# Four edits to a two-layer decoder trunk: where the index queries are split, what S3 is summed from, how fast weight sums are issued, where residual rows are scaled

## The chip, the cores and the metric

The kernel runs on one core of a Trainium2 chip. The metric is the device time of one execution, in microseconds (us). Five engines with an instruction queue each matter here: TensorE (PE in the profile; PEld are its weight loads), VectorE (DVE), ScalarE (ACT), GpSimd (POOL) and SyncE (SP). Each engine works through its own queue in order; an instruction whose semaphore has not come blocks everything queued behind it on that engine. Transfers are issued by SP (queue q1 in the profile) and by POOL (queue q0) and are carried out by the same 16 DMA engines.

## The reference

Two layers (DEPTH = 2) over 512 positions of width 2048, all in float32:

```python
h = jnp.einsum('bsd,dn->bsn', x, w_in)              # one projection, its columns split in groups
q_idx = rope(iq.reshape(b, s, 16, 64), pos)         # indexer: 16 query heads, one key head
k_idx = rope(ik.reshape(b, s, 1, 64), pos)[:, :, 0, :]
rel   = relu(einsum('bqhi,bki->bqhk', q_idx, k_idx) * 64 ** -0.5)
score = einsum('bqhk,bqh->bqk', rel, w_idx)         # the 128 best keys of a query are attended to
y = concatenate([y_fox * silu(fg), y_dsa * silu(dg), y_mem * silu(mg)])
x = layer_norm(ALPHA * x + y @ w_out, ln_gain, ln_bias)
```

y_fox is causal attention with a forget bias (6 heads), y_dsa attention over the chosen keys (6 heads), y_mem attention into 256 memory tokens (4 heads). Value, gate and some query columns (5120 of them) and the output projection are by far the largest products.

## The kernel before

Every float32 product is made of three TensorE matmuls: both operands are split into a high and a low part (`split`, L216: ACT copies the high part, `whi`; DVE subtracts to get the low part, `wlo`), and high*high, low*high and high*low are accumulated (`product`, L221, L225 to L227). The weights come in chunks of 128 x 2048 floats, 1 MB each, through six half-chunk buffers `raw`; each half chunk is split once, three halves ahead of its use, into four buffers.

The order of a layer is written out: `mv` and `mk` (memory values and keys), `small` (index key, index weights, forget logits), eight `iq` chunks (two index heads each), 70 `vs` chunks (values), 16 chunks of heads, 28 `out` chunks. An `iq` chunk has 48 matmuls of 384 columns, a `vs` chunk 24 of 512.

The values are a seven-product scheme on 2 x 2 blocks (`PRODUCTS`): P1 = A11 B11, P7 = S3 T3, Q6 = S2 T2, and so on. The left sums S3 = A11 - A21, S2, S1, S4 are made on the core from x (`val_operands`, `val_sum` L848, `val_hi` L853, `val_lo` L859). The right sums T1 to T4 are sums of weight blocks; T3 and part of T1 are made in DRAM by transfers that POOL issues (`weight_sums`: a first copy, L425, then an accumulating transfer, L405, 1 MB each) and loaded later as `raw<-sum`. T2 and T4 are grown in the raw buffers of T3, the first by an accumulating transfer of POOL (`grow_w`, L284), the second by DVE (`make_w`, L294). Ten chunks per column pair come first (P1 P1 P7 P7 P2 Q6 Q6 P2 Q4 Q4, five pairs), then four per pair (Q5 Q5 Q3 Q3).

All other work is in generators that `begin` starts and `tick` advances: once in the middle and once at the end of a chunk, except that those started with `whole=True` skip the middle of `vs` and `out` chunks. So a generator that yields 1 runs at every tick, one that yields 2 at every second one. `paced` decides how many ticks lie between two weight sums, by stage. Outside the value stage each weight sum is preceded by `pool_waits`: DVE writes a mark and POOL reads it, so that POOL can't run ahead. Inside the value stage there is no mark.

After an `iq` chunk, `index_rope` turns the rows (ACT moves four quarters, L588; DVE multiplies, L589 and L590; POOL subtracts, L591), then ACT copies the high part of each of the two heads (L1296) and DVE subtracts (L1297). `index_scores` does one head per tick, from two ticks later: six matmuls (`ix`), three `rel` on ACT (L685), three `acc` on DVE (L691).

Between the layers `next_x` normalises z, transposes it for the next layer (`xf`, `xh`, `xl`; L1034 on DVE and POOL in turns) and stores rows of the residual x1; `residual_rows` in the value stage of the second layer loads rows of x1, multiplies by gain, adds bias (L1052, L1053) and stores them again.

Of the kernel before, what the change touches and what calls it, by code (L numbers as in the profile page):

```python
# [14 lines left out]
ALU = mybir.AluOpType  # L15
# [162 lines left out]
def kernel(  # L178
# [171 lines left out]
    def split_x(k):  # L350
        hi, lo = slot("xh", F32R), slot("xl", F32R)
        split(x_raw.pop(k), hi, lo)
        xT[k] = (hi, lo)

# [73 lines left out]
    def paced(gen, steps=2):  # L428

        n = 0  # L430
        for _ in gen:
            n += 1
            while now[1] == "kv":
                yield 1
            yield {"heads": 1, "out": 3, "index": 1}.get(now[1], steps)
# [10 lines left out]
    def all_sums():  # L446


        for l in range(DEPTH):
            yield from paced(value_sums(l), 1)  # L450
# [218 lines left out]

    def index_scores(l):  # L670
# [189 lines left out]

    def val_operands():
# [3 lines left out]
        for i in range(4):  # L865
            val_sum("S3", i, ((a11, 0, add), (a21, 0, sub), (a11, 1, add), (a21, 1, sub)))
            yield 1
            val_hi("S3", i)
            yield 1
            val_lo("S3", i)  # L870
# [143 lines left out]
    def next_x():  # L1014
# [9 lines left out]
        for k in range(KT):  # L1024
# [10 lines left out]
            xT[k] = (hi, lo)  # L1035
            if k % 2:
                for st in (o - 1, o) if 0 < c < 3 else ():
                    store(st, c - 1)
                if k == 13:
                    load_row(0, 2, nc.sync)  # L1040
                yield 1
        for c in (2, 3):
            for st in range(4):
                if (st, c) == (1, 2):
                    load_row(0, 3, nc.sync)
                scale_row(z[st, c], c)
                store(st, c)
                yield 1
            del rows["g", c], rows["b", c]

    def scale_row(t, c):
        nc.vector.tensor_tensor(t, t, rows["g", c], op=ALU.mult)  # L1052
        nc.vector.tensor_tensor(t, t, rows["b", c], op=ALU.add)  # L1053

    def residual_rows(l):

        tiles = [(st, c) for c in range(2) for st in range(4)]
        t = {}
        for n in range(len(tiles) + 1):
            if n:  # L1060
                st, c = tiles[n - 1]
                d = t.pop(n - 1)
                scale_row(d, c)
# [81 lines left out]
    for i, (kind, l, j, col, _) in enumerate(chunks):  # L1145
# [143 lines left out]
        elif kind == "iq":  # L1289
            t = index_rope(ps, P, P, nc.gpsimd)  # L1290

            for e in range(2):
                s = slot("iqs", F32R)
                r, o = (slice(0, 64), slice(64, 128)) if e == 0 else (slice(64, 128), slice(0, 64))
                c = slice(P, SEQ)
                nc.scalar.activation(s[r, c], t[r, c], AF.Copy)  # L1296
                nc.vector.tensor_tensor(s[o, c], t[r, c], s.bitcast(F32)[r, c], op=ALU.subtract)  # L1297
                idx["q", 2 * j + e] = s
            if j == 0:
                begin(index_scores(l), 2, last=True, whole=True)  # L1300
            if j == 2:
                begin(val_operands(), 2, last=True)
# [149 lines left out]
```

## Time and profile before

| what | us |
|---|---|
| median of 3 runs (lowest to highest) | 1953.41 (1953.16 to 1954.32) |
| profiled execution, its time | 1953.65 |
| its span, first to last instruction | 1951.8 |
| PE busy | 1905.0 (98%) |
| DVE busy | 1475.0 (76%) |
| ACT busy | 1015.8 (52%) |
| POOL busy | 367.4 (19%) |
| all transfers | 499.35 MB |

A busy PE is not PE at full speed: matmuls overlap, and the granted clock (PEclk, 1.00 is full speed) can be lower. The share of the DMA engines is the time that packets took over the time of 16 engines, so it can be a little over 1.

In the span, layer 0 has its `iq` chunks from about 60 to 145 us and its values from there to about 545; layer 1 has them from about 1040 to 1125 and to about 1505.

### The profile page before, as it was taken

How to read it: one execution, taken by the hardware profiler on the slowest of the kernel's cores; microseconds unless marked ns; L12 is line 12 of the kernel's file. 1: busy time of each engine (PE TensorE's matmuls, PEld its weight loads, DVE VectorE, ACT ScalarE, POOL GpSimd, SP SyncE). 2: the span in 40 equal slices, each digit the busy share in tenths (PEclk: the TensorE clock that was granted, in tenths of full speed). 3: DMA queues.
4: the chain of work that ended last, by engine and by line, in shares of the span. 5: the costliest groups of instructions: out<-in, count | busy, mean ns of one | idle time of the engine just before them, and what ended most of it. 6: DMA issues, size and time to landing. Idle time of an engine off the chain costs nothing.

```text
span 1951.8 us, 26382 instructions
## 1 busy us (share of the span) xinstructions
PE 1905.0 (98%) x9250; PEld 1616.7 (83%) x9250; DVE 1475.0 (76%) x2422; ACT 1015.8 (52%) x1598; POOL 367.4 (19%) x618
## 2 busy tenths in 40 slices
PE   9998899999999999999999989999999999999997
PEld 8996678888888888888899968888888888888886
DVE  5788477777955676789787887898877466767888
ACT  5665244445455554555474664444554565455453
POOL 0223111111122122110042221111212220112101
PEclk9999899999999999999999989999999999999999
DMA  9899886688987789798888997877999886889965
GB/s 342 285 282 237 271 253 181 181 225 265 342 275 223 233 249 278 227 335 270 299 251 283 283 220 222 252 238 210 230 278 340 265 241 201 263 252 252 348 199 152
DMA packets 168115, 499.35 MB, mean 256 GB/s; under 512 B 16865, under 2 KB 61921, under 8 KB 159085
## 3 DMA queue, kind: packets, MB, share of 16 engines
q1 hardware_dynamic: 131724, 294.19, 44.4%
q0 software_dynamic: 36256, 203.47, 40.8%
q8 instruction: 73, 1.20, 0.2%
q14 instruction: 62, 0.50, 0.1%
HBM read 451.43 MB, written 174.09 MB: 320 GB/s over the span
## 4 chain that ended last, share of the span: by engine, by line
PE 81%; DVE 10%; ACT 3%; DMA 3%; issue 2%; POOL 1%; SPq 0%; DVEq 0%; ACTq 0%; POOLq 0%
PE v L226 12%; PE v L227 12%; PE v L225 12%; PE c L227 8%; PE c L225 7%; PE c L226 7%; PE z L226 4%; PE z L227 4%; PE z L225 4%; DVE wlo L219 3%; DMA raw<-in_wall_dram 2%; DVE acc L691 1%; DMA raw<-sum 1%; ACT whi L218 1%; DVE vx L848 1%
## 5 line engine op out<-in xcount | busy, mean ns | idle before, releaser
L219 DVE TENSOR_TENSOR wlo<-raw,whi 128x1024 fp32r<-128x1024 f32 (+1 forms) x521 | 636.0, 1225 | 272.8 <-ACT whi L218 270.7
L218 ACT ACTIVATE whi<-raw 128x1024 fp32r<-128x1024 f32 (+1 forms) x521 | 548.0, 1054 | 438.8 <-PE v L227 247.3
L225 PE MATMUL c<-xh,whi 128*128 128x512 f32 (+1 forms) x800 | 301.4, 377 | 0.6 <-ACT rel L685 0.6
L227 PE MATMUL c<-xh,wlo 128*128 128x512 f32 (+1 forms) x800 | 298.4, 373 | 0.0
L226 PE MATMUL c<-xl,whi 128*128 128x512 f32 (+1 forms) x800 | 297.8, 372 | 0.0
L226 PE MATMUL v<-wlo,vxh 128*128 128x512 f32 x640 | 249.4, 390 | 2.3 <-DVE wlo L219 2.3
L225 PE MATMUL v<-whi,vxh 128*128 128x512 f32 x640 | 249.7, 390 | 1.2 <-ACT whi L218 1.2
L227 PE MATMUL v<-whi,vxl 128*128 128x512 f32 x640 | 249.1, 389 | 0.0
L226 PE MATMUL v<-wlo,xh 128*128 128x512 f32 x480 | 192.7, 401 | 11.8 <-DVE wlo L219 7.6
L225 PE MATMUL v<-whi,xh 128*128 128x512 f32 x480 | 191.3, 399 | 9.9 <-ACT whi L218 9.9
L227 PE MATMUL v<-whi,xl 128*128 128x512 f32 x480 | 191.3, 399 | 0.0
L226 PE MATMUL z<-wlo,yh 128*128 128x512 f32 (+1 forms) x434 | 168.1, 387 | 2.5 <-DVE wlo L219 2.5
L225 PE MATMUL z<-whi,yh 128*128 128x512 f32 (+1 forms) x434 | 168.4, 388 | 0.0
L227 PEld LDWEIGHTS c<-xh,wlo 128*128 128x128 f32 x800 | 150.1, 188 | 21.9
L225 PEld LDWEIGHTS c<-xh,whi 128*128 128x128 f32 x800 | 150.3, 188 | 21.5 <-ACT rel L685 1.2
L227 PE MATMUL z<-whi,yl 128*128 128x512 f32 (+1 forms) x434 | 167.8, 387 | 0.0
L226 PEld LDWEIGHTS c<-xl,whi 128*128 128x128 f32 x800 | 150.4, 188 | 20.6
L396 POOL TENSOR_TENSOR seen<-mark,mhalf 128x1 f32<-128x1 f32 x107 | 28.0, 261 | 700.2 <-DVE mark L395 689.5
L226 PEld LDWEIGHTS v<-wlo,vxh 128*128 128x128 f32 x640 | 120.1, 188 | 27.9 <-DVE wlo L219 3.2
L225 PEld LDWEIGHTS v<-whi,vxh 128*128 128x128 f32 x640 | 120.1, 188 | 27.2 <-ACT whi L218 2.3
L227 PEld LDWEIGHTS v<-whi,vxl 128*128 128x128 f32 x640 | 120.1, 188 | 25.0
L226 PEld LDWEIGHTS v<-wlo,xh 128*128 128x128 f32 x480 | 92.8, 193 | 33.7 <-DVE wlo L219 14.4
(226 smaller groups left out, 3207.6 us busy)
## 6 DMA issues: line engine op xcount, KB each, us to landing
raw<-in_wall_dram SPq DMA_DIRECT2D x322, 512.0 KB, 7.4
sum<-in_wall_dram POOLq DMA_DIRECT2D x60, 1024.0 KB, 11.6
raw<-sum SPq DMA_DIRECT2D x120, 512.0 KB, 6.4
v<-vraw POOLq DMA_DIRECT2D x120, 256.0 KB, 6.3
raw<-in_wall_dram POOLq DMA_DIRECT2D x48, 512.0 KB, 8.0
vraw<-v SPq DMA_DIRECT2D x80, 256.0 KB, 6.6
other<-in_wall_dram SPq DMA_DIRECT2D x48, 256.0 KB, 9.1
x<-z POOLq DMA_DIRECT2D x24, 256.0 KB, 5.6
```

The source lines that it names most:

```text
L218: nc.scalar.activation(hi, src, AF.Copy)
L219: nc.vector.tensor_tensor(lo, src, hi.bitcast(F32), op=ALU.subtract)
L225: nc.tensor.matmul(ps, ah, bh, start=start, stop=False, skip_group_check=more)
L226: nc.tensor.matmul(ps, ah, bl, start=False, stop=False, skip_group_check=more)
L227: nc.tensor.matmul(ps, al, bh, start=False, stop=stop, skip_group_check=more)
L396: nc.gpsimd.tensor_tensor(seen, mark, mhalf, op=ALU.mult)
L691: nc.vector.scalar_tensor_tensor(a, rel, wq, a, op0=ALU.mult, op1=ALU.add)
L848: nc.vector.tensor_tensor(d, acc, x, op=op)
```

## The change

- `index_parts` is new: the ACT copies and DVE subtractions of the two index heads leave the end of the `iq` chunk and come as a generator with a wait of 1, at the tick in the middle of the next chunk.
- `first_sum` is new: S3 is one subtraction per 256 columns from the unsplit x (`xraw` in layer 0, `xf` in layer 1), issued where x is split. Before, it was summed from the split parts in `val_operands`, three operations per 256 columns. Its high and low parts come from `first_operands`, started after the first `iq` chunk; `val_operands` (S2 first) starts after the last `iq` chunk, not the third.
- Weight sums for the values: one per two ticks instead of one per tick, in the index and in the value stage. The pace in the heads and out stages stays.
- `next_x` stores all 16 tiles of x1 unscaled, the last four over two ticks; `residual_rows` scales all 16 and not 8, and starts at the first pair's second Q6 chunk and not the second pair's, ten chunks earlier.

```diff
@@ -349,8 +349,10 @@
 
     def split_x(k):
         hi, lo = slot("xh", F32R), slot("xl", F32R)
-        split(x_raw.pop(k), hi, lo)
+        x = x_raw.pop(k)
+        split(x, hi, lo)
         xT[k] = (hi, lo)
+        first_sum(k, x)
 
     load_w(0, 4)
     load_w(1, 2)
@@ -432,7 +434,7 @@
             n += 1
             while now[1] == "kv":
                 yield 1
-            yield {"heads": 1, "out": 3, "index": 1}.get(now[1], steps)
+            yield {"heads": 1, "out": 3, "index": 2}.get(now[1], steps)
 
     def value_sums(l):
 
@@ -447,7 +449,7 @@
 
 
         for l in range(DEPTH):
-            yield from paced(value_sums(l), 1)
+            yield from paced(value_sums(l))
             while now != (l, "heads"):
                 yield 1
             yield from paced(weight_sums("out", l, ("T3", "T1", "T2", "T4"), range(2)))
@@ -667,6 +669,17 @@
                                     pattern=[[-1, P]], channel_multiplier=1)
         yield 1
 
+    def index_parts(j, t):
+
+        for e in range(2):
+            s = slot("iqs", F32R)
+            r, o = (slice(0, 64), slice(64, 128)) if e == 0 else (slice(64, 128), slice(0, 64))
+            c = slice(P, SEQ)
+            nc.scalar.activation(s[r, c], t[r, c], AF.Copy)
+            nc.vector.tensor_tensor(s[o, c], t[r, c], s.bitcast(F32)[r, c], op=ALU.subtract)
+            idx["q", 2 * j + e] = s
+        yield 1
+
     def index_scores(l):
         acc = [slot("acc", w=w) for w in BANK_W]
         kh2, kl2 = idx["k"]
@@ -858,16 +871,26 @@
         t = vx[name, i] if name == "S3" else vx.pop((name, i))
         nc.vector.tensor_tensor(lo, t, hi.bitcast(F32), op=ALU.subtract)
 
+    def first_sum(k, x):
+
+        i, e = divmod(k, 2)
+        if i < 4:
+            if e == 0:
+                vx["S3", i] = slot("vx")
+            nc.vector.tensor_tensor(vx["S3", i][:, e * 256:(e + 1) * 256], x[:, 0:256], x[:, 256:512],
+                                    op=ALU.subtract)
+
+    def first_operands():
+        for i in range(4):
+            val_hi("S3", i)
+            yield 1
+            val_lo("S3", i)
+            yield 1
+
     def val_operands():
         add, sub = ALU.add, ALU.subtract
         a11, a12, a21, a22 = (0, 0), (0, 1), (1, 0), (1, 1)
 
-        for i in range(4):
-            val_sum("S3", i, ((a11, 0, add), (a21, 0, sub), (a11, 1, add), (a21, 1, sub)))
-            yield 1
-            val_hi("S3", i)
-            yield 1
-            val_lo("S3", i)
         for i in range(4):
             val_sum("S2", i, (("S3", 0, add), (a22, 0, add), (a22, 1, add)), vx.pop(("S3", i)))
             yield 1
@@ -1033,34 +1056,26 @@
             eng = nc.gpsimd if k % 2 else nc.vector
             eng.tensor_tensor(lo, xf, hi.bitcast(F32), op=ALU.subtract)
             xT[k] = (hi, lo)
+            first_sum(k, xf)
             if k % 2:
-                for st in (o - 1, o) if 0 < c < 3 else ():
+                for st in (o - 1, o) if c else ():
                     store(st, c - 1)
-                if k == 13:
-                    load_row(0, 2, nc.sync)
                 yield 1
-        for c in (2, 3):
-            for st in range(4):
-                if (st, c) == (1, 2):
-                    load_row(0, 3, nc.sync)
-                scale_row(z[st, c], c)
-                store(st, c)
+        for st in range(4):
+            store(st, 3)
+            if st % 2:
                 yield 1
-            del rows["g", c], rows["b", c]
-
-    def scale_row(t, c):
-        nc.vector.tensor_tensor(t, t, rows["g", c], op=ALU.mult)
-        nc.vector.tensor_tensor(t, t, rows["b", c], op=ALU.add)
 
     def residual_rows(l):
 
-        tiles = [(st, c) for c in range(2) for st in range(4)]
+        tiles = [(st, c) for c in range(4) for st in range(4)]
         t = {}
         for n in range(len(tiles) + 1):
             if n:
                 st, c = tiles[n - 1]
                 d = t.pop(n - 1)
-                scale_row(d, c)
+                nc.vector.tensor_tensor(d, d, rows["g", c], op=ALU.mult)
+                nc.vector.tensor_tensor(d, d, rows["b", c], op=ALU.add)
                 nc.gpsimd.dma_start(x1_d[st * P:(st + 1) * P, c * 512:(c + 1) * 512], d)
                 if st == 3:
                     del rows["g", c], rows["b", c]
@@ -1289,17 +1304,12 @@
         elif kind == "iq":
             t = index_rope(ps, P, P, nc.gpsimd)
 
-            for e in range(2):
-                s = slot("iqs", F32R)
-                r, o = (slice(0, 64), slice(64, 128)) if e == 0 else (slice(64, 128), slice(0, 64))
-                c = slice(P, SEQ)
-                nc.scalar.activation(s[r, c], t[r, c], AF.Copy)
-                nc.vector.tensor_tensor(s[o, c], t[r, c], s.bitcast(F32)[r, c], op=ALU.subtract)
-                idx["q", 2 * j + e] = s
+            begin(index_parts(j, t), 1)
             if j == 0:
                 begin(index_scores(l), 2, last=True, whole=True)
-            if j == 2:
-                begin(val_operands(), 2, last=True)
+                begin(first_operands(), last=True)
+            if j == 7:
+                begin(val_operands(), 3, last=True)
             if j == 7:
                 index_tabs.clear()
         if kind in ("fk", "dk"):
@@ -1316,7 +1326,7 @@
             now = (l, "values")
         if kind == "vs" and (name, pair, col) == ("Q6", 0, 1):
             begin(top_keys(l), whole=True)
-        if kind == "vs" and (name, pair, col) == ("Q6", 1, 1) and l > 0:
+        if kind == "vs" and (name, pair, col) == ("Q6", 0, 1) and l > 0:
             begin(residual_rows(l), whole=True)
         if kind == "vs" and (name, col) == ("Q3", 1) and pair > 1:
             if pair == 2:
```

With the change, one chunk of the index stage of layer 0 reads so on DVE. In these rows `wlo` is the low part of a weight half chunk, `iqs` an index head's low part, `acc` the scores of 256, 384 and 512 keys, `vx` the sum S3, `vxl` its low part, `rope` the rotation. Before, from the two `iqs` of the fifth `iq` chunk on:

```order
L1297 TENSOR_TENSOR iqs_1400<-rope_1391,iqs_1400 64x384
L1297 TENSOR_TENSOR iqs_1403<-rope_1391,iqs_1403 64x384
L395 COPY mark_1406<-mhalf 128x1
L691 SCALAR_TENSOR_TENSOR acc_1014<-rel_1421,iw_845,acc_1014 128x256
L691 SCALAR_TENSOR_TENSOR acc_1013<-rel_1424,iw_845,acc_1013 128x384
L691 SCALAR_TENSOR_TENSOR acc_1015<-rel_1427,iw_845,acc_1015 128x512
L859 TENSOR_TENSOR vxl_1361<-vx_1297,vxh_1360 128x512
L848 TENSOR_TENSOR vx_1431<-xh_503 128x256
L848 TENSOR_TENSOR vx_1431<-vx_1431,xl_504 128x256 x2
L848 TENSOR_TENSOR vx_1431<-xh_507 128x256
L848 TENSOR_TENSOR vx_1431<-vx_1431,xl_508 128x256 x2
L219 TENSOR_TENSOR wlo_1444<-raw_1307,whi_1443 128x1024
```

And with the change, in the middle of the fourth `iq` chunk, from a weight half chunk on:

```order
L219 TENSOR_TENSOR wlo_1174<-raw_1039,whi_1173 128x1024
L679 TENSOR_TENSOR iqs_1201<-rope_1132,iqs_1201 64x384
L679 TENSOR_TENSOR iqs_1204<-rope_1132,iqs_1204 64x384
L704 SCALAR_TENSOR_TENSOR acc_1013<-rel_1216,iw_857,acc_1013 128x256
L704 SCALAR_TENSOR_TENSOR acc_1012<-rel_1219,iw_857,acc_1012 128x384
L704 SCALAR_TENSOR_TENSOR acc_1014<-rel_1222,iw_857,acc_1014 128x512
L872 TENSOR_TENSOR vxl_1166<-vx_557,vxh_1165 128x512
L219 TENSOR_TENSOR wlo_1227<-raw_1169,whi_1226 128x1024
L591 TENSOR_TENSOR rope_1254<-c_1168,tab_715 128x384
L592 TENSOR_TENSOR rope_1255<-rope_1255,tab_717 128x384
L397 COPY mark_1270<-mhalf 128x1
L704 SCALAR_TENSOR_TENSOR acc_1013<-rel_1284,iw_857,acc_1013 128x256
```

The six `vx` additions are gone from this place, and the two `iqs` stand behind a weight half chunk and no longer right behind the rotation that they read.

The second place is POOL in the value stage of layer 0, at the end of the first column pair. `sum` from `16x16384` is the first copy of a weight sum, `sum` from `128x2048` the accumulating transfer, `v` a store of values. Before:

```order
L425 DMA sum_2127<-in_wall_dram 16x16384
L425 DMA sum_2166<-in_wall_dram 16x16384
L425 DMA sum_2207<-in_wall_dram 16x16384
L956 DMA v_163<-vraw_2201 128x512
L956 DMA v_163<-vraw_2074 128x512
L956 DMA v_163<-vraw_2204 128x512
L956 DMA v_163<-vraw_2076 128x512
L405 DMA sum_2078<-in_wall_dram 128x2048
L956 DMA v_162<-vraw_2248 128x512
L956 DMA v_162<-vraw_2250 128x512
L405 DMA sum_2127<-in_wall_dram 128x2048
L405 DMA sum_2166<-in_wall_dram 128x2048
```

With the change:

```order
L427 DMA sum_2102<-in_wall_dram 16x16384
L979 DMA v_163<-vraw_2137 128x512
L979 DMA v_163<-vraw_2001 128x512
L979 DMA v_163<-vraw_2140 128x512
L979 DMA v_163<-vraw_2003 128x512
L407 DMA sum_1512<-in_wall_dram 128x2048
L979 DMA v_162<-vraw_2182 128x512
L979 DMA v_162<-vraw_2184 128x512
L407 DMA sum_1630<-in_wall_dram 128x2048
L979 DMA v_162<-vraw_1871 128x512
L979 DMA v_162<-vraw_1873 128x512
```

Around the same eight stores there are three sums and not seven, and the runs of sums with nothing between them are gone. All 28 sums of the layer are still issued, the last of them some 40 value chunks into the stage and not some 12.

The third place is DVE between the layers, where `next_x` splits the new x (`xl`). Before:

```order
L1034 TENSOR_TENSOR xl_9313<-xf_9311,xh_9312 128x512
L219 TENSOR_TENSOR wlo_9333<-raw_9268,whi_9332 128x1024
L1034 TENSOR_TENSOR xl_9355<-xf_9353,xh_9354 128x512
L219 TENSOR_TENSOR wlo_9371<-raw_9328,whi_9370 128x1024
L1034 TENSOR_TENSOR xl_9393<-xf_9391,xh_9392 128x512
```

With the change:

```order
L1057 TENSOR_TENSOR xl_9265<-xf_9263,xh_9264 128x512
L880 TENSOR_TENSOR vx_9269<-xf_9263 128x256
L880 TENSOR_TENSOR vx_9269<-xf_9276 128x256
L219 TENSOR_TENSOR wlo_9288<-raw_9220,whi_9287 128x1024
L1057 TENSOR_TENSOR xl_9310<-xf_9308,xh_9309 128x512
L880 TENSOR_TENSOR vx_9314<-xf_9308 128x256
```

Two subtractions of S3 stand now behind every second `xl`, eight per layer.

## The prediction

> **What bounds the kernel now.** I read the table of stages first (busy time of each engine, granted clock, share of the DMA engines, rate), because the page shows PE busy for 98% of the span and the question is where the rest is lost.
>
> ```profile
> core 0: us, PE busy (x) PEld busy (x) DVE busy (x) ACT busy (x) POOL busy (x), PEclk, DMA share, GB/s
> 80.00:145.00 65.00, 65.00 (x377) 63.50 (x376) 54.00 (x113) 42.70 (x80) 20.75 (x32) 1.00 0.94 274
> 145.00:190.00 45.00, 36.92 (x155) 29.21 (x155) 39.38 (x67) 27.91 (x47) 15.83 (x24) 0.92 0.97 234
> 190.00:262.00 72.00, 58.55 (x221) 44.56 (x220) 34.52 (x50) 20.98 (x23) 11.57 (x16) 0.91 0.95 269
> 262.00:400.00 138.00, 138.00 (x611) 114.25 (x610) 112.58 (x162) 63.37 (x68) 19.05 (x30) 1.00 0.70 204
> 1070.00:1152.00 82.00, 73.00 (x371) 65.89 (x371) 67.29 (x128) 51.76 (x97) 21.28 (x35) 0.94 0.93 260
> 1152.00:1232.00 80.00, 80.00 (x356) 66.45 (x355) 64.46 (x92) 40.56 (x49) 14.07 (x21) 1.00 0.81 210
> 1232.00:1330.00 98.00, 98.00 (x434) 81.13 (x433) 85.17 (x125) 44.64 (x48) 20.16 (x32) 1.00 0.83 249
> ```
>
> PE is full in most stages; three lose time, and those are where the change works. Idle plus clock deficit: 145 to 190 us loses 8.1 + 45 x 0.08 = 11.7 us, 1070 to 1152 us loses 9.0 + 82 x 0.06 = 13.9 us. From 190 to 262 us I count matmuls, all of one width there: 611 in 138 us is 0.226 us each, so 221 are 49.9 us of work and 22.1 us are lost. Together 47.7 us, the most that can be won here.
>
> Second, who makes PE wait in the two stretches, 140 to 265 us and 1050 to 1155 us:
>
> ```profile
> PE v L225 <- ACT whi L218: 10.9, 6, 4.3
> PE v L226 <- DVE wlo L219: 7.1, 7, 2.8
> PE v L226 <- DVE mark L395: 2.1, 1, 2.1
> ...
> PE ix L680 <- DVE iqs L1297: 3.9, 3, 1.7
> PE v L226 <- DVE wlo L219: 2.8, 1, 2.8
> ```
>
> So PE waits for split weights: in layer 1 for DVE, in layer 0 also for ACT's half. Third, the chain of waits between 185 and 262 us, with its two longest pieces, says why ACT was late there:
>
> ```profile
> 191.49 19.84 DMA raw<-in_wall_dram
> ...
> 226.94 23.62 DMA raw<-sum
> ```
>
> There the weights themselves arrived late. Two causes, then: DVE before 190 us and in layer 1, transfers from 190 to 262 us.
>
> **The change part by part.** *Index stage, DVE.* The groups of 75 to 165 us (count, busy us, mean ns, idle before them):
>
> ```profile
> L219 DVE TENSOR_TENSOR wlo<-raw,whi 128x1024 fp32r<-128x1024 f32 x16 | 19.5, 1218 | 1.8 <-ACT whi L218 1.8
> L691 DVE SCALAR_TENSOR_TENSOR acc<-rel,iw,acc 128x512 f32<-128x512 f32 x12 | 8.9, 745 | 0.0
> L1297 DVE TENSOR_TENSOR iqs<-rope,iqs 64x384 fp32r<-64x384 f32 x16 | 8.9, 554 | 14.3 <-ACT iqs L1296 14.1
> L1296 ACT ACTIVATE iqs<-rope 64x384 fp32r<-64x384 f32 x16 | 8.4, 524 | 21.8 <-POOL rope L591 21.6
> L848 DVE TENSOR_TENSOR vx<-vx,xl 128x256 f32<-128x256 f32 x18 | 7.7, 425 | 0.6
> L691 DVE SCALAR_TENSOR_TENSOR acc<-rel,iw,acc 128x384 f32<-128x384 f32 x12 | 7.3, 611 | 0.0
> L691 DVE SCALAR_TENSOR_TENSOR acc<-rel,iw,acc 128x256 f32<-128x256 f32 x12 | 5.7, 475 | 0.0
> L589 DVE TENSOR_TENSOR rope<-c,tab 128x384 f32<-128x384 f32 x8 | 4.4, 550 | 0.8 <-ACT rope L588 0.8
> L590 DVE TENSOR_TENSOR rope<-rope,tab 128x384 f32<-128x384 f32 x8 | 4.4, 546 | 0.0
> L848 DVE TENSOR_TENSOR vx<-xh 128x256 f32<-128x256 f32 x8 | 3.3, 418 | 0.0
> L859 DVE TENSOR_TENSOR vxl<-vx,vxh 128x512 fp32r<-128x512 f32 x4 | 2.7, 685 | 0.0
> ```
>
> PE needs 60 matmuls per `iq` chunk (48, and 6 for each of two heads): 60 of 377 in 65 us is 10.3 us. DVE needs two `wlo` (2.44), rotation (1.10), two `iqs` (1.11), two rounds of `acc` (3.66): 8.3 us. From the fourth chunk on, S3 adds six `vx` (2.54) and a `vxl` (0.69), and every chunk adds 14.3 / 8 = 1.8 us of waiting at `iqs`, since DVE stands behind ACT, which stands behind POOL: 13.3 us against 10.3. DVE falls some 3 us behind per chunk until the four buffers of split weights are used up, near 145 us.
>
> The change takes 24 of these `vx` (24 x 0.42 = 10.1 us) out of each layer's index stage and puts the `iqs` pair half a chunk (5 us) later, behind a `wlo`, when POOL's 1 us subtraction is long done. What is left is 8.3 us, 9.0 while `vxl` lasts: below 10.3, so DVE no longer falls behind. S2 (16 additions and four low parts of 0.69, about 9.5 us) now starts only in the second value chunk. DVE there per chunk: 2.44 + 1.83 (last heads) + 1.7 (S2) + 0.69 = 6.6 us, against 24 matmuls and one head, 5.4 + 1.0 = 6.4; it starts with full buffers, so nothing is lost. The first operands of Q6 are ready about one chunk (5.4 us) before use; if that cover were gone, each of Q6's four half chunks could wait up to one S2 step, 2.4 us. I take 11 of the 11.7 us in layer 0 and all but nothing, 14 with the small losses around it, in layer 1 (from 8, if `iqs` waits stay, to 14).
>
> The 8 new subtractions (8 x 0.42 = 3.4 us) run in the memory stage. In layer 0 DVE has room. Between the layers it has little: `wlo` there is stretched
>
> ```profile
> L219 DVE TENSOR_TENSOR wlo<-raw,whi 128x1024 fp32r<-128x1024 f32 x10 | 14.6, 1458 | 1.6 <-ACT whi L218 1.6
> ```
>
> (985 to 1015 us: 1458 ns and not 1218, beside POOL's half of `xl`), with 1.6 us idle in 30. 3.4 us of more work there meets buffered weights; cost 0 to 3 us, I take 0.5, because PE never waited there.
>
> *Weight sums.* Queue q0 from 60 to 150 us carried almost nothing but sums:
>
> ```profile
> q0 software_dynamic: 1110, 14.48, 57.2%
> ```
>
> 90 us x 0.572 / 14.48 MB is 3.56 us of all engines per MB, 3.7 us for a sum of 1 MiB. A value chunk without sums needs 0.70 x 5.4 = 3.8 us (262 to 400 us above). Before, a sum per chunk made this 7.5 us per 5.4: transfers are the bound until the 28 sums are through. Issue to landing, 190 to 262 us, then 262 to 400 us:
>
> ```profile
> sum<-in_wall_dram POOLq DMA_DIRECT2D x4, 1024.0 KB, 21.3
> raw<-sum SPq DMA_DIRECT2D x4, 512.0 KB, 18.6
> raw<-in_wall_dram POOLq DMA_DIRECT2D x4, 512.0 KB, 15.2
> ...
> raw<-sum SPq DMA_DIRECT2D x12, 512.0 KB, 5.6
> raw<-in_wall_dram POOLq DMA_DIRECT2D x8, 512.0 KB, 7.4
> ```
>
> With half the pace it is 3.8 + 1.85 = 5.65 us per 5.4, 104%, for 40 chunks. Taken at its word that is an excess of 9 us; none, if the engines can do 1.06, as they do here with PE full:
>
> ```profile
> 500.00:550.00 50.00, 50.00 (x222) 41.42 (x221) 40.27 (x55) 24.24 (x27) 12.64 (x16) 1.00 1.06 338
> ```
>
> With six buffers of half a chunk (2.7 us) each a load has up to 16 us from issue to split, and the runs of sums without a store between them are shorter now. I keep 5 of the 22.1 us (0 to 9, all 22 in a rival) and gain 17. Nothing waits for the sums themselves: pair p needs its T3 at about value chunk 10p, and its last transfer is issued 4 ticks (pair 0) to 17 chunks (pair 4) before the load; T1 is done at tick 55 and loaded at 66. In the index stage the halving also takes out eight marks of 0.15 us; the transfers there cost PE nothing (65.0 of 65 us).
>
> *Residual rows.* A tile costs two DVE operations:
>
> ```profile
> L1052 DVE TENSOR_TENSOR z<-z,row x16: 679/682/693, 1023.3 to 1323.8; 128x512 f32<-128x512 f32 x16
> L1053 DVE TENSOR_TENSOR z<-z,row x16: 691/692/693, 1024.0 to 1324.5; 128x512 f32<-128x512 f32 x16
> ```
>
> Eight tiles (11 us) leave 1023 to 1052 us, where PE was full: no gain. They join layer 1's values, with a load on SP, a store on POOL each and four rows on SP. DVE with rows is 85.2 of 98 us (1232 to 1330 us), 87% and no wait of PE; the longer stretch stays at that. The DMA share goes up by 0.13 (0.83 against 0.70), 0.7 us per chunk, and for some 16 chunks rows and half-paced sums now overlap: 3.8 + 1.85 + 0.7 = 6.35 us per 5.4, 117%, an excess of 15 us. It can be carried by the 16 us that a load has, and drains once the sums end; 0 to 15, I take 5.
>
> Sum against the profiled execution's 1953.65 us (span 1951.8; the median of the runs is 1953.41, no different): - 11 - 14 - 17 + 0.5 + 5 = -36.5, so **1917 us**.
>
> One rule bears on the prices of what is left. Three stalled stretches ran at granted clocks of 0.91 to 0.94, 15 of the 47.7 us, so I priced left-over stalls with the clock in them. The Trainium skill, "TensorE: Matmul & The Clock Gate", section "What's actually happening", says that TensorE falls to half its clock after an idle window of about 3.4 us. By that rule short left-over waits would cost idle time alone, about two thirds of my 10 us, and the sum would be 1914.
>
> **The rivals.** *Nothing new is lost* (transfers at 104 and 117% are carried by prefetch): 1953.65 - 47.7 = 1906. For it: PE full at a share of 1.06. Against: that stretch is mostly SP's loads, not sums.
>
> *The transfer stall only moves.* If any sum in flight slows the loads as much as many do, 40 chunks of sums cost as much as 20: layer 0 keeps its 22 us, the gain is 25 - 5.5: 1934. For it: 104%. Against: `raw<-sum` 18.6 us with sums bunched, while in 60 to 150 us, with a sum per 5 us, PE lost nothing. The Trainium skill, "DMA: Bandwidth & Descriptors", section "Queues, rings and completion order", has each DMA engine take turns between the queues that have work, a packet at a time; by that rule it matters whether q0 has work at all, not how much, which speaks for this rival and against the change.
>
> *The index heads become the wait.* PE's `ix` already waited for `iqs` (3.9 us in three waits in layer 1), and the change takes half a chunk off its lead. If DVE does not catch up, eight heads per layer wait 1.7 us, 27 us in all: 1944. Against: rotation (1.1), `acc` (1.8), `wlo` (1.2) and some 2 us of ACT's quarters stand before `iqs` (1.1), so they are done some 7 us after the chunk's end, and PE needs them at 10.3.
>
> *Slower: the grown weights.* Q6's weights are grown by POOL's transfers, in one queue with the sums, and have 13.5 us (five halves) to be split, about 21 to be used. Were their landing, 15.2 us at its worst, to reach 30 us behind two sums and the row stores, each of six column pairs (four in layer 0, two in layer 1) would lose 9 us: 54, against 47 saved: 1961. It decides from about 29 us of landing time. Against: in 190 to 262 us, with more sums queued, it was 15.2.
>
> **How the numbers follow.** The forecast, 1908 to 1928: 0.55. Nothing lost (1906): 0.20. The stall moves (1934): 0.15. Heads: 0.06. Grown weights: 0.04. The range, 1903 to 1937, takes in the first three cases, whose bounds are 1903 (every term at its best, and some 3 us of small waits around the stretches won too) and 1937. A difference of 0.2% (4 us) is what the measurement tells from none. Only the last rival, and a part of the heads' case, is not faster: faster 0.94, same 0.02, slower 0.04.
>
> **What would show it.** Right: idle before `iqs` on DVE near zero, clock 1.00 through both index stages, `wlo` waits of PE gone at the entry to the values; layer 0's first 120 us of values with a share near 1.0 and single waits of PE for `whi`, a few us in all; landing of `raw<-sum` around 8 to 12 us; layer 1's values with rows and sums the place of new waits. Wrong: PE waits for `iqs` in every chunk; landing of 20 us spread over 40 chunks; PE waiting between the layers; a loss in layer 1's values beyond 15 us.

## The result, and the profile after

The changed kernel takes 1937.33 us (median of 4 runs, 1935.36 to 1938.20), the kernel before on the same chip 1953.29: a ratio of 0.9918, 95% interval 0.9901 to 0.9935. It is faster, by 16 us and not by 36; the time lies just past the upper end of the range, 1937 us. The profiled execution took 1935.36 us, 18.3 less than the one before.

The table of stages after the change (columns as in the prediction):

```profile
85.00:145.00 60.00, 60.00 (x349) 58.59 (x348) 51.40 (x82) 43.88 (x81) 14.12 (x20) 1.00 0.69 202
145.00:220.00 75.00, 75.00 (x339) 62.63 (x339) 59.54 (x89) 38.76 (x53) 18.01 (x28) 1.00 0.87 235
220.00:325.00 105.00, 98.16 (x413) 77.54 (x412) 75.31 (x110) 43.07 (x48) 19.55 (x30) 0.98 0.88 260
325.00:400.00 75.00, 74.36 (x329) 61.24 (x328) 58.92 (x83) 32.20 (x35) 16.01 (x22) 1.00 1.01 283
985.00:1055.00 70.00, 68.27 (x449) 65.28 (x447) 47.25 (x72) 44.85 (x73) 24.65 (x31) 1.00 0.77 266
1055.00:1140.00 85.00, 85.00 (x449) 78.19 (x449) 74.39 (x115) 60.28 (x105) 22.60 (x30) 1.00 0.80 199
1140.00:1200.00 60.00, 59.38 (x262) 48.84 (x261) 46.23 (x67) 23.91 (x26) 12.87 (x21) 1.00 0.99 311
1200.00:1285.00 85.00, 76.13 (x310) 60.21 (x309) 66.64 (x100) 33.46 (x36) 16.76 (x27) 0.94 0.88 262
```

Before, in the same cut, the stretches of the values that matter:

```profile
145.00:220.00 75.00, 58.84 (x228) 45.60 (x228) 52.78 (x83) 36.07 (x56) 18.55 (x29) 0.89 0.92 247
220.00:325.00 105.00, 99.64 (x425) 80.31 (x425) 72.57 (x108) 42.12 (x45) 16.72 (x24) 0.98 0.82 225
1055.00:1140.00 85.00, 78.36 (x426) 72.61 (x425) 66.90 (x138) 53.01 (x100) 22.21 (x38) 0.98 0.89 260
1200.00:1285.00 85.00, 85.00 (x377) 70.38 (x376) 67.50 (x99) 38.34 (x41) 13.64 (x20) 1.00 0.80 220
```

A loss in the values is counted in matmuls from here on: undisturbed (the run without sums below) the stretches from 145 us hold 340, 465 and 333, those from 1140 us 266, 376 and 509, at 0.226 us each. Layer 0 was 152 short before (34.4 us) and is 57 short now (12.9 us). Both index stages are full at clock 1.00 in these rows: the 13.9 us that the prediction counted in layer 1 are gone. But layer 1's values, full before from 1152 us on, now miss 70 matmuls (4 and 66), 15.8 us, and 1.7 us are idle between the layers. 21.5 + 13.9 - 15.8 - 1.7 is 17.9 us, against 18.3.

DVE did in the index stage what was forecast. The two index groups of 75 to 165 us, with the idle before them (14.3 and 21.8 us before):

```profile
L679 DVE TENSOR_TENSOR iqs<-rope,iqs 64x384 fp32r<-64x384 f32 x16 | 8.9, 554 | 0.5
L678 ACT ACTIVATE iqs<-rope 64x384 fp32r<-64x384 f32 x16 | 8.4, 524 | 2.6 <-POOL rope L593 2.4
```

PE's waits, in layer 0's values (140 to 400 us), in layer 1's (1130 to 1300 us) and, last row, over the whole span, and two pieces of the chain of waits (195 to 325 us):

```profile
PE v L226 <- DVE wlo L219: 5.0, 8, 0.8
PE v L225 <- ACT whi L218: 2.3, 2, 1.5
...
PE v L226 <- DVE wlo L219: 5.8, 6, 2.3
PE v L225 <- ACT whi L218: 3.7, 2, 3.6
...
PE ix L693 <- DVE iqs L679: 2.4, 2, 1.3
```
```profile
210.16 20.69 DMA raw<-in_wall_dram
...
270.07 18.88 DMA raw<-in_wall_dram
```

PE waits for split weights again, and behind them stand loads of about 20 us, as long as before. The stall on transfers is spread, not gone. The issues of 60 to 148 us, then of 148 to 460 us (two rows for sums: accumulating transfers, with 1024.0 KB, and first copies, without a size):

```profile
sum<-in_wall_dram POOLq DMA_DIRECT2D x2, 1024.0 KB, 8.3
sum<-in_wall_dram POOLq DMA_DIRECT2D x6, 5.8
...
sum<-in_wall_dram POOLq DMA_DIRECT2D x12, 1024.0 KB, 12.8
raw<-sum SPq DMA_DIRECT2D x24, 512.0 KB, 12.8
sum<-in_wall_dram POOLq DMA_DIRECT2D x8, 13.9
```

8 of layer 0's 28 sums are issued before the values begin, 20 after. Meanwhile the index stage moves data for 0.69 of its time.

### The profile page after: what moved, and what is told of

Read it like the earlier page. It is cut to its first block, busy times and chain, and to the rows that moved or that the text cites. A ratio compares the mean times of both kernels' runs of the same rounds, so it can differ in the third digit from the quotient of the medians.

```text
span 1933.6 us, 26367 instructions
## 1 busy us (share of the span) xinstructions
PE 1898.5 (98%) x9250; PEld 1612.4 (83%) x9250; DVE 1469.4 (76%) x2374; ACT 1016.7 (53%) x1598; POOL 372.9 (19%) x610
## 4 chain that ended last, share of the span: by engine, by line
PE 70%; DMA 11%; DVE 11%; ACT 4%; issue 2%; POOL 1%; SPq 0%; DVEq 0%; ACTq 0%; POOLq 0%
DMA raw<-in_wall_dram 10%; PE v L226 8%; PE v L227 8%; PE v L225 8%; PE c L227 8%; PE c L225 8%; PE c L226 8%; DVE wlo L219 4%; PE z L226 4%; PE z L227 4%; PE z L225 4%; ACT whi L218 2%; PE pt L776 1%; DVE raw L294 1%; PE ix L693 1%
## 5 line engine op out<-in xcount | busy, mean ns | idle before, releaser
L398 POOL TENSOR_TENSOR seen<-mark,mhalf 128x1 f32<-128x1 f32 x91 | 23.6, 259 | 620.3 <-DVE mark L397 611.6
L226 PEld LDWEIGHTS v<-wlo,xh 128*128 128x128 f32 x480 | 91.3, 190 | 31.9 <-DVE wlo L219 12.9
## 6 DMA issues: line engine op xcount, KB each, us to landing
sum<-in_wall_dram POOLq DMA_DIRECT2D x60, 1024.0 KB, 11.6
```

The lines of the kernel that those rows point to most:

```text
L226: nc.tensor.matmul(ps, ah, bl, start=False, stop=False, skip_group_check=more)
L398: nc.gpsimd.tensor_tensor(seen, mark, mhalf, op=ALU.mult)
```

## The experiments

All times are medians; the kernel before took 1952.4 to 1952.9 us beside them.

| run | us | ratio to before (95%) |
|---|---|---|
| changed, rows as before | 1936.66 | 0.9913 (0.9899 to 0.9926) |
| changed, old pace of sums | 1927.12 | 0.9868 (0.9854 to 0.9881) |
| changed, old pace in the index stage only | 1918.33 | 0.9821 (0.9808 to 0.9834) |
| changed, no sums | 1907.34 | 0.9766 (0.9753 to 0.9780) |
| before, index queries alone | 1940.66 | 0.9940 (0.9928 to 0.9953) |
| before, S3 alone | 1937.16 | 0.9922 (0.9908 to 0.9935) |
| before, pace alone | 1959.16 | 1.0031 (1.0019 to 1.0043) |
| changed, old index pace, one sum in four in the values | 1907.31 | 0.9767 (0.9754 to 0.9780) |
| the last one, rows as before | 1911.65 | 0.9787 (0.9774 to 0.9800) |
| changed, one sum in three in the values | 1924.04 | 0.9848 (0.9834 to 0.9861) |
| before, one sum in four in the values | 1930.79 | 0.9889 (0.9875 to 0.9902) |
| before, rows alone | 1950.51 | 0.9988 (0.9979 to 0.9997) |

**Rows as before.** The edit gives back the eight tiles to the stretch between the layers and starts the rest later:

```diff
...
-        if kind == "vs" and (name, pair, col) == ("Q6", 0, 1) and l > 0:
+        if kind == "vs" and (name, pair, col) == ("Q6", 1, 1) and l > 0:
             begin(residual_rows(l), whole=True)
```

> The changed kernel with the residual rows where they were before (eight tiles scaled between the layers, the other eight from the second column pair's Q6); everything else as changed. Theory (layer 1's new loss of some 16 us between 1155 and 1290 us comes from rows and weight sums running beside each other): that loss falls to 4 us or less, 1923 to 1926 us. Rival (half-paced sums do it alone, as they do in layer 0, where there are no rows): layer 1 keeps 12 us or more of it, 1933 to 1938 us.

1936.66 us, no change: by its time the rival, but the stages show two effects that cancel.

```profile
985.00:1055.00 70.00, 65.34 (x414) 62.47 (x413) 54.13 (x82) 41.27 (x64) 23.38 (x31) 0.95 0.79 278
1200.00:1285.00 85.00, 78.16 (x330) 62.28 (x329) 64.73 (x96) 32.99 (x36) 15.79 (x25) 0.98 0.86 248
```
```profile
PE ix L693 <- DVE iqs L679: 3.5, 1, 3.5
```

Layer 1's values lose 47 matmuls (10.6 us) and not 70: the rows edit costs 5.2 us there, and the rest is lost with the rows as before (half-paced sums beside eight tiles, which no run takes apart). Between the layers 4.7 us are idle and the clock is 0.95, where the changed kernel had 1.7 idle at 1.00: with eight tiles to scale there, DVE is late for the first index query, which PE awaits for 3.5 us and not 1.3.

**Old pace.**

```diff
-            yield {"heads": 1, "out": 3, "index": 2}.get(now[1], steps)
+            yield {"heads": 1, "out": 3, "index": 1}.get(now[1], steps)
...
-            yield from paced(value_sums(l))
+            yield from paced(value_sums(l), 1)
```

> The changed kernel with the weight sums at the pace of before (one per chunk, in the index stage and in the values). Theory (transfers decide in the first 120 us of the values, and the half pace won the 8 us that layer 0 shows, 22 down to 14): layer 0 loses 22 us again between 190 and 262 us; in layer 1 the sums are through earlier and meet fewer of the rows, so that its 16 us fall to about 8: 1935 to 1939 us. Rival (the pace does nothing in layer 0, its 8 us came from DVE's earlier lead): layer 0 stays at 14, layer 1 falls: 1925 to 1931 us. Second rival (in layer 1 more sums at once beside the rows cost more): 1945 us or more.

1927.12 us, 10 less than the changed kernel: the rival's time, though not its reason. Layer 0 loses 80 matmuls (18.1 us, 5 more than the changed kernel, between the theory's 22 and the rival's 14), so the pace does act there; but layer 1 loses only 11 from 1140 us on (2.5 us, 13 less), much less than the theory's 8 us:

```profile
145.00:220.00 75.00, 70.93 (x311) 56.78 (x310) 55.90 (x82) 35.38 (x50) 21.02 (x31) 1.00 1.02 291
220.00:325.00 105.00, 98.40 (x415) 79.41 (x414) 75.66 (x110) 44.73 (x49) 14.70 (x22) 0.97 0.77 217
1140.00:1200.00 60.00, 58.47 (x255) 47.44 (x254) 50.90 (x75) 26.79 (x29) 9.62 (x15) 1.00 0.85 262
```

So the half pace as a whole costs 10 us beside the other three edits.

**Old pace in the index stage only.** Of the last diff its first pair of lines alone.

> The changed kernel with one sum per chunk in the index stage (as before) and one in two chunks in the values (as changed): some five sums more are through when the values begin. Theory (the index stage has unused transfer time, a share of 0.71 at 80 to 145 us with PE full, so a sum there is free, and what a layer loses in its values follows the number of sums left): 28 sums lose 14 us in layer 0 with some 22 left for the values, so 17 left lose 3 to 4 us less in each layer: 1929 to 1932 us. Rival (the loss does not hang on the number of sums, but on the single column pairs whose loads have no slack): 1936 to 1938 us. Second rival (sums in the index stage bring back waits there): over 1940 us.

1918.33 us, 19 less than the changed kernel; the theory had expected 5 to 8 less. It had counted one sum per chunk there; the stage has two steps per chunk, so that 16 sums (6 + 10) and not 8 are issued before the values:

```profile
sum<-in_wall_dram POOLq DMA_DIRECT2D x6, 1024.0 KB, 13.5
...
sum<-in_wall_dram POOLq DMA_DIRECT2D x10, 10.5
```
```profile
85.00:145.00 60.00, 60.00 (x348) 58.55 (x348) 51.76 (x86) 44.50 (x84) 20.80 (x32) 1.00 1.00 291
145.00:220.00 75.00, 71.50 (x311) 58.70 (x310) 59.43 (x89) 37.52 (x52) 18.36 (x28) 0.95 0.96 278
220.00:325.00 105.00, 103.18 (x453) 84.40 (x452) 77.63 (x112) 45.03 (x50) 17.80 (x26) 1.00 0.86 246
1200.00:1285.00 85.00, 85.00 (x377) 70.38 (x376) 74.72 (x112) 38.85 (x42) 19.29 (x32) 1.00 0.84 275
```

The index stage has a share of 1.00 and PE is full: the eight sums are free there. Layer 1, where 3 sums are issued from 1104 to 1300 us against 11 in the changed kernel, loses nothing, with all sixteen rows in its values. Layer 0 loses 41 matmuls, 9.3 us. Halving in the index stage costs 19 us, halving in the values wins 9 (1927 to 1918).

**No sums.**

```diff
-                        if n:
+                        if kind == "val":
+                            if not n:
+                                sums[key] = src
+                        elif n:
                             add_weights(key, src)
```

> The changed kernel without the transfers of the values' weight sums; the products that multiply with a sum load the first of its two terms instead (so part of the weights that the values are computed with is left out). The loads keep their number, size and queue. Theory (the sums' transfers make the loads late): layer 0's 14 us go to 2 or less, and layer 1's 16 us, with the rows left alone at 0.13 of the share, to 4 or less: 1908 to 1913 us. Rival (the loads are late through the holding of buffers for the grown weights, sums or not): at least half of the 30 us stays, 1922 us or more.

1907.34 us. Both layers' values are full:

```profile
220.00:325.00 105.00, 105.00 (x465) 86.95 (x464) 82.14 (x118) 46.47 (x50) 14.30 (x24) 1.00 0.67 194
1200.00:1285.00 85.00, 85.00 (x376) 70.38 (x375) 74.09 (x108) 39.03 (x42) 16.88 (x26) 1.00 0.86 272
```

The theory: all 30 us are the sums' transfers. Holding buffers for grown weights costs nothing by itself, nor do the rows (a share of 0.86).

**Index queries alone, S3 alone,** each on the kernel before (the two parts of the diff as the change has them).

```diff
-            for e in range(2):
-                s = slot("iqs", F32R)
...
+            begin(index_parts(j, t), 1)
```

> The kernel before with one part of the change: the index queries' two parts made half a chunk behind the rotation (S3, pace and rows as before). Theory of the prediction (DVE needs 8.3 us per index chunk, 3.2 us more for S3 from the fourth chunk on, and 1.8 us more of waiting at the index queries; PE needs 10.3): without the waiting 11.5 us against 10.3, some 6 us behind at the end, which four buffers of split weights nearly hold. Most of 11.7 us in layer 0 and of 14 us in layer 1 is won, 18 to 23 us: 1930 to 1935 us. Rival (S3's additions are what matters, the waiting is slack of an engine that is not the bound): under 8 us won, 1945 us or more.

```diff
...
-            if j == 2:
-                begin(val_operands(), 2, last=True)
+                begin(first_operands(), last=True)
+            if j == 7:
+                begin(val_operands(), 3, last=True)
```

> The kernel before with another part of the change: S3 summed from x unsplit in the memory stage, S2 begun in the second value chunk (index queries, pace and rows as before). Theory of the prediction: 8.3 + 0.7 + 1.8 = 10.8 us of DVE and waiting per index chunk against PE's 10.3, nearly in balance, so that most of the 25 us is won here too, 19 to 25 us: 1928 to 1934 us, and the two single gains together are more than the 26 us that the changed kernel with the old pace won. Rival (the waiting at the index queries grows as DVE gets less behind, and takes the gain): under 10 us won, 1943 us or more.

1940.66 and 1937.16 us: 12 and 15 us won, each below what was expected, and together 27, about the 26 of the old-pace run (which has the rows too). The gains add; that each takes its own part of DVE's lag fits this, and was not shown apart. A part of what the index queries alone fell short by is a new wait between the layers (1000 to 1070 us), before the layer's first index query:

```profile
PE ix L691 <- DVE iqs L677: 3.7, 1, 3.7
```

With a clock of 0.98 over these 70 us it costs some 5 us. There are no S3 subtractions in that run. With S3 alone, PE waits 0.6 us for that query and 0.7 us for a split weight there. So the wait came with the later index queries and not with the subtractions.

**Pace alone,** on the kernel before: the pace lines of the change.

> The kernel before with the half pace of the weight sums alone, in the index stage and in the values. The prediction's term: 17 us won in layer 0, 5 lost in layer 1 at most: 1936 to 1941 us. Theory after the first four runs (halving in the index stage, where transfers cost nothing, costs 19 us, because it leaves some eight more sums of each layer for the values; halving in the values wins 9): 1955 to 1965 us. Rival (in the kernel before, DVE's own stalls give the transfers time, so that neither shows): 1951 to 1955 us.

1959.16 us: slower, by 0.31% (0.19 to 0.43%). The prediction's term for this edit (1936 to 1941) falls; the theory after the first four runs holds. The entry to the values is better than before (283 matmuls, not 228), the rest of layer 0 and layer 1 worse (340, not 377):

```profile
145.00:220.00 75.00, 68.80 (x283) 55.56 (x284) 62.70 (x98) 39.81 (x60) 17.13 (x27) 0.93 0.78 205
220.00:325.00 105.00, 97.83 (x408) 76.56 (x407) 67.73 (x97) 40.99 (x46) 17.07 (x24) 0.98 0.88 256
1200.00:1285.00 85.00, 81.31 (x340) 65.00 (x339) 58.18 (x88) 35.86 (x40) 17.18 (x24) 0.96 0.99 278
```

**One sum in four value chunks,** with the index stage at its old pace:

```diff
-            yield {"heads": 1, "out": 3, "index": 2}.get(now[1], steps)
+            yield {"heads": 1, "out": 3, "index": 1}.get(now[1], steps)
...
-            yield from paced(value_sums(l))
+            yield from paced(value_sums(l), 4)
```

> The changed kernel with one sum per step of the index stage (as before) and one in four value chunks (changed: one in two). Theory (what is left of the loss, 9 us in layer 0 with one sum in two value chunks and none in layer 1, comes from sums that are in flight while the second P2 chunk of a column pair, whose load has no slack, is fetched): with half as many sums there at any time about half of the 9 us goes, 1912 to 1915 us. Rival (the loss at the entry to the values comes from the sums still queued from the index stage, whose share is 1.02, and from the grown weights): 1917 to 1920 us, no difference. Second rival (a sum comes too late for its load): a new wait for a load, 1925 us or more.

1907.31 us, as fast as without any sum, and the best version here: 2.3% below the kernel before. The 9 us of layer 0 shrink to 6 matmuls (1.4 us):

```profile
145.00:220.00 75.00, 74.31 (x334) 61.54 (x334) 62.40 (x92) 40.30 (x55) 17.66 (x26) 1.00 0.93 260
220.00:325.00 105.00, 105.00 (x465) 86.91 (x465) 81.17 (x118) 47.10 (x50) 17.85 (x28) 1.00 0.81 249
985.00:1055.00 70.00, 68.33 (x418) 65.03 (x417) 47.74 (x84) 45.95 (x78) 20.16 (x33) 1.00 0.93 308
```

**The same with rows as before** (the diff of the first experiment on this version).

> The fastest version so far (the changed kernel with one sum per step of the index stage and one in four value chunks, 1907 us) with the residual rows where they were before the change. With the half pace, undoing the rows changed nothing: layer 1's values lost some 5 us less, but 5 us more were lost at 1010 to 1060 us, where PE waited 3.7 us for the first index query and its clock was 0.91. Theory (both sides are real: rows cost transfers in the values, DVE time between the layers): with the sums out of the way only the second side is left, 1911 to 1914 us. Rival (the two differences were chance of one profile): 1906 to 1909 us.

1911.65 us. With transfers out of the way the rows edit is worth 4.3 us (0.2% by the ratios), as the theory had it; the best version has 68.33 and not 65.92 us of PE in this stretch, at a clock of 1.00, and waits 1.5 and not 3.6 us for the first index query:

```profile
985.00:1055.00 70.00, 65.92 (x391) 62.39 (x390) 56.36 (x94) 42.32 (x70) 18.45 (x30) 0.98 0.93 312
```

**One sum in three value chunks,** the index stage at the half pace. At this pace some sums are loaded before their second term has been added, so that part of the weights is left out of the values; loads and transfers keep number and size.

```diff
-            yield from paced(value_sums(l))
+            yield from paced(value_sums(l), 3)
```

> The changed kernel with one sum in three value chunks (changed: one in two); the index stage stays at the half pace. Theory (the sum of transfer times decides: 3.8 us of a chunk without sums, 1.85 us of a sum in two chunks is 104% of 5.4 us, 1.23 us of a sum in three is 93%, although 20 sums of layer 0 are left for the values and not 12): the loss of 14 and 16 us goes to 5 or less in each layer, 1909 to 1917 us. Rival (what counts is how many sums are left at the entry to the values, whatever their pace, since each takes a slice from loads without slack): at least 20 of the 30 us stay, 1927 us or more. Second rival (a sum of column pair 2 comes too late for its load): one long wait, 1920 to 1930 us.

1924.04 us, by its time the second rival, but no wait of that kind: layer 0 is full to 400 us, with as many sums left (20) as in the changed kernel. Later it loses 6.6 us (326 matmuls from 440 to 520 us, 355 in the best version), where the last sums are in flight beside the loads of weight pairs (a share of 1.06), and layer 1 loses 47 matmuls (10.6 us) where sums meet rows:

```profile
220.00:325.00 105.00, 105.00 (x465) 86.94 (x465) 81.14 (x118) 46.79 (x50) 19.74 (x30) 1.00 0.87 256
440.00:520.00 80.00, 77.07 (x326) 62.76 (x325) 57.57 (x79) 33.83 (x40) 11.39 (x13) 0.96 1.06 326
1200.00:1285.00 85.00, 81.30 (x347) 65.56 (x346) 69.35 (x104) 32.62 (x36) 21.89 (x34) 0.98 0.97 285
1285.00:1400.00 115.00, 112.06 (x491) 91.41 (x490) 98.25 (x145) 55.97 (x64) 21.32 (x32) 1.00 0.84 244
```

So the number of sums left does not count by itself; the transfer time per chunk does. With 93% of a chunk nothing is lost in layer 0 to 400 us, where neither weight pairs nor rows come in.

**Before, one sum in four value chunks.**

```diff
-            yield from paced(value_sums(l), 1)
+            yield from paced(value_sums(l), 4)
```

> The kernel before with one sum in four value chunks as the only edit (the index stage at its pace of before, none of the edits to DVE's work). Theory (the stall from 190 to 262 us, 22 us, is transfers alone, and DVE's 11.7 us before it and 14 to 17 us in layer 1 are another cause): 18 to 22 us are won, 1931 to 1935 us. Rival (the stall at 190 to 262 us comes from DVE being behind at the entry, so that buffers come free late and loads start late): under 10 us won, 1943 us or more.

1930.79 us, 22 won, just past the theory's end. The transfer stall is gone whole; DVE's losses stay:

```profile
145.00:220.00 75.00, 69.14 (x286) 56.16 (x287) 65.17 (x101) 41.18 (x61) 16.94 (x27) 0.93 0.91 244
220.00:325.00 105.00, 105.00 (x465) 86.97 (x464) 80.53 (x118) 47.76 (x51) 18.05 (x28) 1.00 0.80 239
1055.00:1140.00 85.00, 76.32 (x379) 68.17 (x378) 72.01 (x136) 52.47 (x97) 20.98 (x33) 0.94 0.94 257
```

Layer 0: 54 matmuls, 12.2 us; layer 1: 8.7 idle and 0.06 of 85 us in the clock, 13.8 us.

**Before, rows alone** (the rows' part of the diff).

> The kernel before with the residual rows alone changed (all sixteen tiles scaled in layer 1's values). Theory (the 4.3 us that this edit is worth beside the other edits exist only because the eight new S3 subtractions load DVE in the same stretch between the layers; the prediction's zero for the rows and 0.5 us for the subtractions were right for each alone, not for the two together): no gain here, 1950 to 1956 us. Rival (taking eight tiles from DVE between the layers lets it enter the index stage ahead, which is worth something by itself): 1945 to 1949 us. Second rival (rows and sums at the old pace collide in layer 1's values): 1957 us or more.

1950.51 us, 0.12% less (0.03 to 0.21%), below what the prediction called a difference. Of the 4.3 us 1.8 are there on the kernel before; between the layers nothing could be won, since PE was full there, and still is. The theory gave the rest to the S3 subtractions. The run with the index queries alone says otherwise: the wait of 3.7 us that the rows edit shortens is there without them.

```profile
985.00:1055.00 70.00, 70.00 (x453) 65.01 (x452) 48.20 (x59) 46.62 (x68) 25.71 (x29) 1.00 0.84 279
```

## Why the prediction was right in its causes and wrong in its time

| term | predicted | measured |
|---|---|---|
| index stage, layer 0 | -11 | -10.8: 12.2 us with the transfers eased alone, 1.4 with DVE's edits too |
| index stage, layer 1 | -14 | -13.8: as much is left with the transfers eased alone, nothing with DVE's edits |
| transfer stall, layer 0: "I keep 5 of the 22.1" | -17 | -9.2: 12.9 us are left |
| eight subtractions between the layers | +0.5 | +0.5, a wait for a split weight |
| first index query between the layers | no term | +1.3 |
| rows beside half-paced sums: "0 to 15, I take 5" | +5 | +15.8 |
| sum | -36.5 | -16.2, against 16 by the medians, 18.3 by the profiles |

*Right:* two causes, DVE and transfers, and their split. Eased alone, transfers give back 22 us (1930.79) as the 22.1 counted; the index and S3 edits, with the rows, give 26 (1927.12) where their terms and the subtractions give 24.5. The bound without new losses, 1906 us, is reached to within 2 us by two kernels (1907.34 and 1907.31). Signs announced came: almost no idle time of DVE before `iqs`, clock 1.00 in the index stages, rows with sums the place of new waits. `raw<-sum` lands in 12.8 us, just past "8 to 12", and the share of layer 0's values is 0.87 and 0.88 to 325 us, where one near 1.0 was announced. Two signs of being wrong came too: PE waits between the layers, and the loss in layer 1's values, 15.8 us, is past the 15 that was named.

*The step that failed* is the one from arithmetic to cost: "It can be carried by the 16 us that a load has". The prediction had 104% of a chunk in layer 0 and 117% where rows join, excesses of 9 and 15 us at their word, and took 5 for each. Measured: 12.9 and 15.8 (of these 10.6 with the rows as before). The same arithmetic, a chunk without sums taking 3.8 us of 5.4 and a sum 3.7, holds over the runs, within about half of its size: 93% of a chunk lost 0 us in layer 0 to 400 us, 87% (one sum in four) 1.4; 104% for the 24 chunks that 12 sums take, an excess of 6, lost 9.3; 139% (one per chunk) for 12 chunks, 25, lost 18.1. Of the cases with an excess, only the last lost less than it, by 7 us; in the others the loads' lead carried none of it. It was priced as if the lead of a load renewed itself; that it is spent once fits these figures, but no run followed the lead of single loads. The arithmetic is one of averages: over pieces of 10 us the share in layer 0's values of the changed kernel goes from 0.32 (300 to 310 us, where PE waits) to 1.14 (170 to 180 us, where it doesn't). It does not cover the 6.6 us that one sum in three lost from 440 to 520 us.

*What the prediction saw and did not use:* "the transfers there cost PE nothing" was said of the index stage, as a reason why the halving is harmless there. It is the reason why it is harmful: eight sums per layer were taken out of a stage with a full PE at a share of 0.94 to 1.00 and put where a chunk had no room. That is 19 us, more than the half pace in the values won.

*The rivals.* "The transfer stall only moves" (1934) came nearest in time, and for layer 0 it is half right (12.9 of 22 stay). Its mechanism, any sum in flight slows the loads as much as many do, is refuted: one sum in three or four leaves layer 0 full, or all but full, to 400 us. The rule of the Trainium skill, "DMA: Bandwidth & Descriptors", section "Queues, rings and completion order", was read as speaking for it (whether POOL's queue has work, not how much); these runs do not bear that reading out. Heads and grown weights did not appear as they were priced: PE waits for `iqs` twice, 2.4 us in all, once per layer, and the grown weights land in 8.8 us in layer 0's values and 13.0 in layer 1's (medians).

*A cost without a term.* The prediction took 0.5 us for the subtractions, and 0.5 us is what PE waits for a split weight between the layers. It counted that no head would wait, and had no term for the layer's first index query, which the index edit makes later while DVE has other work in the same stretch: 3.7 us with that edit alone, 1.3 in the changed kernel. It took nothing for the rows between the layers. Alone, they win 1.8 us; beside the other edits 4.3, since fewer tiles then stand between DVE and that query: the rows edit pays for a cost of the index edit.

*Left-over stalls.* I priced them with the clock in them. The run bears that out: in layer 1's worst stretch 8.9 us are idle and 0.06 of 85 us, 5.1, are clock. The Trainium skill, "TensorE: Matmul & The Clock Gate", section "What's actually happening", by whose idle window of about 3.4 us short waits should cost idle time alone, does not hold here as I read it: some 3.4 of the 5.1 us follow PE's wait of 3.6 us (a clock of 0.83 from 1200 to 1220 us), which the rule allows for, but 1.8 follow a wait of 2.3 us (below).

## What to carry to other kernels

Before slowing background transfers down, ask of every stage whether it has room: a stage whose bounding engine stays full at a DMA share of 1.0 is the place to put them, and a pace should be high there and low where loads have little lead (here one per step in the index stage, one in four chunks in the values: 1907 us). Work out transfer time per step of the bounding engine; above about 100% take the whole excess as lost (here 0.7 to 1.6 times it was), and don't count on prefetch to carry it. Cost two edits that add and remove work in the same stretch together.

## What the runs showed of the hardware that was not expected

A high DMA share is no sign of a stall, nor a lower one of room. With a share of 1.00 the index stage had PE full; with 0.88 layer 1's values lost 15 us in 85. A likely reason, not followed load by load, is that while PE waits no buffer comes free and fewer loads are issued, so that a stall lowers the share of the stretch that it is in.

Short waits can cost clock too. Three stretches of 20 us of the changed kernel, with PE's waits in the first:

```profile
1270.00:1290.00 20.00, 17.69 (x70) 13.91 (x69) 19.51 (x30) 7.44 (x8) 5.06 (x10) 0.91 0.76 269
220.00:240.00 20.00, 17.51 (x74) 13.42 (x73) 13.05 (x19) 8.86 (x11) 3.56 (x5) 1.00 1.04 295
300.00:320.00 20.00, 17.89 (x70) 13.75 (x69) 14.84 (x22) 8.28 (x9) 4.30 (x8) 0.91 0.65 222
```
```profile
PE v L226 <- DVE wlo L219: 2.3, 1, 2.3
```

One wait of 2.3 us (1270 to 1290 us) was followed by a granted clock of 0.91 over 20 us, 1.8 us more: nearly the wait again. About the same idle time in waits of at most 1.5 us left the clock at 1.00 from 220 to 240 us, while from 300 to 320 us 2.1 us in waits of at most 0.8 us cost as much clock as the one wait of 2.3 us. So the length of the single wait does not decide it; what does, these runs do not show.
